# Scores of a chunked scan: the causal mask moved into the exponent, written by a fill and an accumulating transfer

## The chip, the core and the metric

The kernel runs on one core of a Trainium2 chip. A core has a matrix engine (TensorE, PE in the profile; its weight loads are PEld), a vector engine (VectorE, DVE), an activation engine (ScalarE, ACT), GpSimd (POOL) and SyncE (SP). SP, ACT and POOL each issue transfers (DMAs) in the order of their own instructions, and sixteen DMA engines that all of them share move the data. The metric is the device time of one execution in microseconds. Lower is better.

## What is computed

One layer of a hybrid decoder: token mixing by causal pooling and by a Mamba-2 scan side by side, gated and merged, then an MLP. 512 tokens plus 16 meta tokens, width 1024, everything in float32. The part that matters here is the scan, cut to its diagonal part and its output:

```python
a_cs = jnp.cumsum(a_dt, axis=2)                       # running sums within a chunk of 128
mask = jnp.tril(jnp.ones((CHUNK, CHUNK), dtype=bool))[:, :, None, None]
diff = a_cs[:, :, :, None] - a_cs[:, :, None, :]
lmat = jnp.exp(jnp.where(mask, diff, -jnp.inf))
cb = jnp.einsum("bclgn,bcsgn->bclsg", cf, bf)
y_diag = jnp.einsum("bclsg,bclsgr,bcsgrp->bclgrp", cb, lmat, xdt)
...
y_off = jnp.einsum("bclgn,bcgrpn,bclgr->bclgrp", cf, prev, jnp.exp(a_cs))
y = (y_diag + y_off).reshape(bsz, lp, SSM_HEADS, SSM_HEAD_DIM)[:, pad:]
```

For every pair of positions l >= s in a chunk, the score is `cb` times the exponential of the difference of two running sums; for l < s it is zero. There are 8 groups of 4 heads and 4 chunks of 128 positions.

## The kernel before

**Stages.** In the profile, the first 61 us are the norm, the step sizes `dt` and the first projections; 61 to 475 us is the scan over the eight groups; after it come the pooling branch, the merge and, from about 690 us, the MLP. Matmuls on TensorE run in a split form (a high and a low part of each float32 operand), which is why a weight block `raw` arrives by SP (L95), is cast by ACT to `whi` (L111) and gives `wlo` by a subtraction on DVE (L113).

**The scan.** For each group g, `ssd(g)` is a generator that computes the scan of that group, and it is woven with `group_proj(g + 1)`, which projects the next group's `bt`, `ct`, `xc` and `z` from weight blocks. `weave` pulls one step of each in turn, and a third generator issues sums of weights on POOL (L774 to L783) behind small marker copies (`seen`, L797); in the first four groups a fourth one forms sums of `u` (`rau`, `rbu`, loaded on POOL at L903, summed by DVE at L911 to L914). The instructions of one engine run in the order in which the framework put them: it plans that order from priorities and estimated durations, within the order that `tc.issue_after` and the helper `after` ask for. An engine that waits for one instruction holds all that are behind it.

**One group's scores.** The tile `abc` has one buffer, 128 partitions x 4 heads x 512 positions, 1 MB. POOL loads the running sums of the group's four heads into it, the same on every partition (L599). The load can start when the previous group's last `py` matmul (L691), which reads that buffer, is done. Then:

- ACT forms `eb = exp(abc)`, two instructions of 64 partitions each, so that the two heads of a pair lie above each other (L633); they stand behind the Silu of `xc` in the first four groups (`x_ready`) and behind that of `z` in the last four (`z_ready`, L584). ACT loads a table when the kind of function changes (`ACT_TABLE_LOAD`): Silu, Sqrt and Exp are of different kinds.
- The difference to the partition's own running sum (`dtok[:, 1]`) is clamped from above at zero: for two heads by ACT with a Relu of the negated difference (L638), for two by DVE with a subtraction and a minimum (L641), in blocks of 128x128.
- `decay` takes the exponentials of both halves (L644, L645). In the last group it stands behind the copy `st0` (L667).
- PE computes `pc`, the products of `bt` and `ct` (L656); DVE multiplies them by `tri`, the 0/1 mask, into `cbm` (L658).
- DVE multiplies the decayed scores by `cbm` over the heads (L676), and PE uses them in `py` (L691), beside `po` (L685), which takes the carried states `st`.
- DVE puts `po * eb + py` and the gates together in `yt` (L694 to L698). ACT squares it (L703) into a tile `sqg` that shares the one buffer of `eb`; its last reader is L331.

`tri` is made once, at the start, by POOL and is 1 where the position of the row is not behind that of the column. `dtok` and its companions are made once in `dt_out`.

Of the kernel before, what the change touches and what calls it, by code (L numbers as in the profile page):

```python
# [11 lines left out]
AF = mybir.ActivationFunctionType  # L12
ALU = mybir.AluOpType

P = 128
# [6 lines left out]
G = 8  # L22
R = 4
# [26 lines left out]
X_PAIRS = (4, 5, 6, 7)  # L50
# [14 lines left out]
def kernel(ctx: ExitStack, tc, xT, x, w, fx, f1, f2, vec, fnw, out):  # L65
    nc = tc.nc
    act, dve, pe, pool = nc.scalar, nc.vector, nc.tensor, nc.gpsimd
# [33 lines left out]
    def after(*ins):  # L101
        st = ExitStack()
        for i in ins:
            if i is not None:
                st.enter_context(tc.issue_after(i.ins))
        return st
# [36 lines left out]
    def mm3s(ps, pairs, first=True, last=True):  # L143
# [4 lines left out]
        for n, ((ah, al), (bh, bl)) in enumerate(pairs):  # L148
# [9 lines left out]
    tri = const.tile([P, P], F32, name="tri")  # L158
    pool.affine_select(out=tri, in_=ones_f, compare_op=ALU.is_ge, fill=0.0, base=0,
                       pattern=[[1, P]], channel_multiplier=-1)  # L160
    eps = const.tile([P, 1], F32, name="eps")
    dve.memset(eps, EPS)
    vs = const.tile([P, V_N], F32, name="vs")
# [5 lines left out]
    dtok = const.tile([P, 2, 4, HEADS], F32, name="dtok")  # L169
# [183 lines left out]
    for i in range(2):  # L353
        pb = psum1(f"pb1_{i}")
        c = slice(3 * i, 3 * i + 3)
# [14 lines left out]
    for c in range(4):  # L370
        r = slice(c * H, (c + 1) * H)
# [22 lines left out]
    acs_d = dram.tile([H, SEQ], F32, name="acs_d")  # L394
    for c in range(4):
        nc.gpsimd.dma_start(acs_d[:, c * P : (c + 1) * P], acs[c * H : (c + 1) * H, :P])
    def dt_out():

        sel = pre.tile([P, 2, P], F32, tag="wdt", name="sel")
        dve.tensor_copy(sel[:, 0, :], ident[:, P - 1 : P].to_broadcast([P, P]))  # L400
        dve.tensor_copy(sel[:, 1, :], ident[:, NM - 1 : NM].to_broadcast([P, P]))
        pt = psum1("pt_dt")
        for j, src in enumerate((dt, acs)):
            pe.transpose(pt[:, j * P : (j + 1) * P], src[:, :P], ident)
            pe.transpose(pt[:NM, 256 + j * H : 256 + (j + 1) * H], src[:H, P:], ident[:H, :H])
        dve.tensor_copy(dtok.rearrange("p a c h -> p (a c h)"), pt[:, :256])
        dve.tensor_copy(dtm.rearrange("p a h -> p (a h)"), pt[:NM, 256 : 256 + 2 * H])
        pq = psum1("pq_dt")
        pe.matmul(pq[:, :128], sel[:, 0, :], dtok[:, 1, :, :].rearrange("p c h -> p (c h)"),
                  start=True, stop=True)  # L410
        pe.matmul(pq[:NM, 128 : 128 + H], sel[:NM, 1, :NM], dtm[:, 1, :], start=True, stop=True)
        fl = lambda t: t.rearrange("p c h -> p (c h)")
        dve.tensor_tensor(fl(dec), pq[:, :128], fl(dtok[:, 1, :, :]), op=ALU.subtract)
        dve.tensor_tensor(wmeta[:NM], pq[:NM, 128 : 128 + H], dtm[:, 1, :], op=ALU.subtract)
        act.activation(fl(dec), fl(dec), AF.Exp)
        act.activation(wmeta[:NM], wmeta[:NM], AF.Exp)
        dve.tensor_tensor(wmeta[:NM], wmeta[:NM], dtm[:, 0, :], op=ALU.mult)
        act.activation(fl(cdec), pq[:, :128], AF.Exp)


    u_d = [dram.tile([P, L], F32, name=f"u_d{k}") for k in range(NK)]
# [10 lines left out]
    x_ready, z_ready, filled = {}, {}, {}  # L432
# [158 lines left out]
    def ssd(g, cur):  # L591

        xc, bt, ct, zt = cur
        hs = slice(R * g, R * g + R)
# [1 line left out]
        ctok = lambda c: slice(c * P, (c + 1) * P)  # L596
        flat = lambda t: t.rearrange("p r d -> p (r d)")
        abc = gs.tile([P, R, SEQ], F32, tag="abc", name=f"abc{g}")
        abc_load[g] = nc.gpsimd.dma_start(abc, acs_d[hs, :].partition_broadcast(P))  # L599

        xdt = gs.tile([P, 4, R, 64], F32, tag="xdt", name=f"xdt{g}")
        btok = gs.tile([P, 4, P], F32, tag="btok", name=f"btok{g}")
# [23 lines left out]
        if g == G - 1:  # L626
            yield
        eb = gs.tile([P, 2, SEQ], F32, tag="eb", name=f"eb{g}")
        ap = abc.rearrange("p (i j) l -> p i j l", j=2)
        for j in range(2):  # L630
            js = slice(64 * j, 64 * j + 64)
            with after((z_ready if g in X_PAIRS else x_ready)[g], late_cast[0] if g == G - 1 else None):
                act.activation(eb[js, :, :], ap[js, :, j, :], AF.Exp)  # L633
        dm = abc.rearrange("p r (c l) -> p r c l", c=4)
        for r in range(R):
            for c in range(4):
                if r < 2:
                    act.activation(dm[:, r, c, :], dm[:, r, c, :], AF.Relu, scale=-1.0,  # L638
                                   bias=dtok[:, 1, c, R * g + r : R * g + r + 1])
                else:  # L640
                    dve.tensor_scalar(dm[:, r, c, :], dm[:, r, c, :], dtok[:, 1, c, R * g + r : R * g + r + 1],  # L641
                                      0.0, op0=ALU.subtract, op1=ALU.min)
        def decay():
            act.activation(abc[:, :2], abc[:, :2], AF.Exp, scale=-1.0)  # L644
            return act.activation(abc[:, 2:], abc[:, 2:], AF.Exp)  # L645


        if g < G - 1:
            done[g] = decay()
        mark[0] = xdt[:, 0, 0, :1]  # L650
        yield

        pc = psum1(f"pcb{g}")
        with tc.issue_after(filled[g].ins) if g in filled else nullcontext():
            for c in range(4):
                pe.matmul(pc[:, c * P : (c + 1) * P], bt[:, tok(c)], ct[:, ctok(c)], start=True, stop=True)  # L656
        cbm = gs.tile([P, 4, P], F32, tag="cbm", name=f"cbm{g}")
        dve.tensor_tensor(cbm, pc.rearrange("p (c l) -> p c l", c=4),  # L658
                          tri.unsqueeze(1).to_broadcast([P, 4, P]), op=ALU.mult)
        st = [gs.tile([P, R, 64], F32, tag=f"st{c}", name=f"st{c}_{g}") for c in range(4)]  # L660
        pss = [psum1(f"pst{g}_{b}") for b in range(2)]
        pv = [pss[c // 2][:, (c % 2) * 256 : (c % 2) * 256 + 256] for c in range(4)]
# [11 lines left out]
        for rs_ in ((slice(0, 2), slice(2, R)) if g == G - 1 else (slice(0, R),)):  # L674
            n = rs_.stop - rs_.start
            masked[g] = dve.tensor_tensor(dm[:, rs_], dm[:, rs_], cbm.unsqueeze(1).to_broadcast([P, n, 4, P]),  # L676
                                          op=ALU.mult)
# [4 lines left out]
        for i in range(2):  # L682
# [5 lines left out]
            for c in range(4):  # L688
                for j in range(2):
                    r = 2 * i + j  # L690
# [937 lines left out]
    c = NC - 1  # L1628
# [203 lines left out]
```

## Time and profile before

| | |
|---|---|
| Median of 3 runs | 1004.51 us (1001.51 to 1004.57) |
| The profiled execution | 1003.26 us, its span 1001.6 us |
| TensorE clock granted | 0.999 |
| PE busy | 989.0 us, 99% of the span |
| DVE / ACT / POOL busy | 804.2 / 602.9 / 121.9 us |
| Moved by DMA | 184.52 MB, mean 184 GB/s |

The profile is one execution. A group row gives line, engine, operation, output<-inputs, shapes and count, then busy time and the mean of one; a row of the timeline gives start, duration, engine, line, operation, and, in brackets, how long the engine stood idle before it and what released it. A row of waits gives who waited for whom: total us, how often, the longest. A row of windows gives the stretch, its length, busy time (and count) of PE, PEld, DVE, ACT and POOL, the granted clock, the share of the DMA engines and GB/s. Matmuls overlap one another, so a PE that counts as busy is close to, but not exactly, a PE at work all the time. The span of a POOL transfer is the time of issuing it; when it has landed is told separately.

### The profile page before, as it was taken

How to read it: one execution, taken by the hardware profiler on the slowest of the kernel's cores; microseconds unless marked ns; L12 is line 12 of the kernel's file. 1: busy time of each engine (PE TensorE's matmuls, PEld its weight loads, DVE VectorE, ACT ScalarE, POOL GpSimd, SP SyncE). 2: the span in 40 equal slices, each digit the busy share in tenths (PEclk: the TensorE clock that was granted, in tenths of full speed). 3: DMA queues.
4: the chain of work that ended last, by engine and by line, in shares of the span. 5: the costliest groups of instructions: out<-in, count | busy, mean ns of one | idle time of the engine just before them, and what ended most of it. 6: DMA issues, size and time to landing. Idle time of an engine off the chain costs nothing.

```text
span 1001.6 us, 15673 instructions
## 1 busy us (share of the span) xinstructions
PE 989.0 (99%) x6035; PEld 873.4 (87%) x6035; DVE 804.2 (80%) x1162; ACT 602.9 (60%) x855; POOL 121.9 (12%) x215
## 2 busy tenths in 40 slices
PE   9999999999999999999999999999999999999997
PEld 7889898989889999978898888888889999999986
DVE  7977997879855888978789667876988878888885
ACT  7657749494924658574345443377666666656654
POOL 0010321211212312223200001121000000000000
PEclk9999999999999999999999999999999999999999
DMA  7374868676798849678823732889354464454332
GB/s 245 89 254 140 265 182 238 195 192 199 221 262 265 232 122 278 211 161 172 286 68 127 252 101 77 259 232 323 88 197 149 142 194 138 157 185 151 129 106 84
DMA packets 61803, 184.52 MB, mean 184 GB/s; under 512 B 7072, under 2 KB 8416, under 8 KB 60704
## 3 DMA queue, kind: packets, MB, share of 16 engines
q1 hardware_dynamic: 39456, 109.00, 33.3%
q0 software_dynamic: 18240, 67.51, 26.4%
q10 hardware_dynamic: 4032, 7.00, 1.9%
q8 instruction: 47, 0.77, 0.3%
q14 instruction: 28, 0.23, 0.1%
HBM read 173.13 MB, written 58.59 MB: 231 GB/s over the span
## 4 chain that ended last, share of the span: by engine, by line
PE 84%; DVE 7%; ACT 4%; DMA 3%; issue 1%; SPq 0%; ACTq 0%; DVEq 0%
PE px L1451 8%; PE px L215 7%; PE alpha L1519 6%; PE pz L215 6%; PE px L1454 4%; PE px L218 4%; PE pgp L215 3%; PE alpha L1522 3%; PE pz L218 3%; PE pgs L215 3%; DMA raw<-in_w 2%; PE pqx L506 2%; PE py L691 2%; PE pgp L218 2%; PE pso L146 1%; PE wo_alpha L1213 1%
## 5 line engine op out<-in xcount | busy, mean ns | idle before, releaser
L113 DVE TENSOR_TENSOR wlo<-raw,whi 128x1024 fp32r<-128x1024 f32 (+2 forms) x88 | 102.2, 1171 | 45.0 <-ACT whi L111 29.7
L111 ACT CAST whi<-raw 128x1024 fp32r<-128x1024 f32 (+2 forms) x88 | 87.2, 1012 | 64.0 <-DMA raw<-in_w 15.8
L215 PE MATMUL px<-uh,whi 128*128 128x264 f32 (+1 forms) x320 | 81.1, 291 | 0.0
L218 PE MATMUL px<-ul,whi 128*128 128x264 f32 (+1 forms) x320 | 78.7, 284 | 0.0
L1226 DVE TENSOR_TENSOR ht<-ht,alpha 128x1024 f32<-128x1024 f32 x35 | 42.7, 1220 | 29.1 <-PE alpha L1519 29.1
L215 PEld LDWEIGHTS px<-uh,whi 128*128 128x128 f32 x320 | 60.5, 189 | 1.1 <-issue 0.9
L1149 ACT CAST shi<-rawf 128x1024 fp32r<-128x1024 f32 x42 | 44.2, 1053 | 28.0 <-PE alpha L1522 18.4
L218 PEld LDWEIGHTS px<-ul,whi 128*128 128x128 f32 x320 | 60.2, 188 | 0.4 <-issue 0.2
L1519 PE MATMUL alpha<-shi,hh 128*128 128x512 f32 x140 | 55.3, 395 | 0.7 <-DVE ht L1226 0.6
L1522 PE MATMUL alpha<-shi,hl 128*128 128x512 f32 x140 | 54.7, 391 | 0.0
L1150 DVE TENSOR_TENSOR slo<-rawf,shi 128x1024 fp32r<-128x1024 f32 x42 | 51.2, 1219 | 0.6 <-ACT shi L1149 0.6
L1454 PE MATMUL px<-vsl,shi 128*128 128x256 f32 x192 | 47.4, 280 | 0.0
L1451 PE MATMUL px<-vsh,shi 128*128 128x256 f32 x192 | 47.4, 281 | 0.0
L215 PE MATMUL pz<-uh,whi 128*128 128x512 f32 x112 | 43.8, 391 | 1.7 <-DVE xc L440 1.7
L218 PE MATMUL pz<-ul,whi 128*128 128x512 f32 x112 | 43.6, 390 | 0.0
L215 PE MATMUL px<-uh,wlo 128*128 128x264 f32 (+1 forms) x320 | 42.0, 283 | 0.0
L215 PEld LDWEIGHTS px<-uh,wlo 128*128 128x128 f32 x320 | 40.0, 188 | 0.0
L1519 PE MATMUL alpha<-slo,hh 128*128 128x512 f32 x140 | 37.4, 389 | 0.0
L1451 PEld LDWEIGHTS px<-vsh,shi 128*128 128x128 f32 x192 | 36.2, 188 | 0.9
L1454 PEld LDWEIGHTS px<-vsl,shi 128*128 128x128 f32 x192 | 36.1, 188 | 0.9
L1454 PE MATMUL px<-vl,shi 128*128 128x256 f32 x144 | 36.1, 283 | 0.0
L1451 PE MATMUL px<-vh,shi 128*128 128x256 f32 x144 | 36.0, 282 | 0.0
(599 smaller groups left out, 3068.3 us busy)
## 6 DMA issues: line engine op xcount, KB each, us to landing
raw<-in_w SPq DMA_DIRECT2D x96, 512.0 KB, 4.6
f_t<-in_f POOLq DMA_DIRECT2D x38, 512.0 KB, 7.5
f_s<-in_f POOLq DMA_DIRECT2D x26, 512.0 KB, 7.0
b<-in_f SPq DMA_DIRECT2D x21, 512.0 KB, 4.4
rawf<-in_f SPq DMA_DIRECT2D x36, 256.0 KB, 3.0
rawf<-f_t SPq DMA_DIRECT2D x36, 256.0 KB, 3.1
abc<-acs_d POOLq DMA_DIRECT2D x8, 1024.0 KB, 8.3
f_t<-f_t POOLq DMA_DIRECT2D x12, 512.0 KB, 6.7
```

Source lines behind the costliest of these rows:

```text
L111: act.copy(hi[:, c], raw[:, c])
L113: dve.tensor_tensor(lo[:, c], raw[:, c], hi[:, c].bitcast(F32), op=ALU.subtract)
L215: pe.matmul(o, wt, rhs[0][k][:, c], start=part == 0 and k == 0, stop=part == 1 and k == NK - 1)
L218: mm[0] = pe.matmul(o, wt, rhs[1][k][:, c], start=False, stop=False)
L506: at = pe.matmul(o, wk, f[k][0], start=start and not low and k == 0, stop=stop and low == 1 and k == 3, skip_group_check=True)
L1149: splits.append((act.copy(hi, src), dve.tensor_tensor(lo, src, hi.bitcast(F32), op=ALU.subtract)))
L1150: dve.tensor_tensor(lo, src, hi.bitcast(F32), op=ALU.subtract)))
L1226: added[0] = dve.tensor_tensor(o, o, src, op=op)
L1451: pe.matmul(ps, m, f[k][0], start=start and not low and k == 0, stop=stop and low == 1 and k == 3, skip_group_check=True)
L1454: pe.matmul(ps, m, f[k][1], start=False, stop=False, skip_group_check=True)
L1519: pe.matmul(ps[t], hh[:, p, seg, st], m, start=bool(first and not low and p == 0), stop=bool(last and low and p == 1), skip_group_check=True)
L1522: pe.matmul(ps[t], hl[:, p, seg, st], m, start=False, stop=False, skip_group_check=True)
```

## The change

The mask goes from a product into the exponent. `tri` becomes 0 where it was 1, and -1e30 where it was 0. For each group POOL first fills `abc` with `tri`, repeated for 4 heads x 4 chunks, from SBUF, and then adds the running sums to it with an accumulating transfer. The sign of the stored own sums (`dtok[:, 1]`) is turned once, so that ACT can take exp(abc + bias) block by block: 16 exponentials with a bias per group take the place of eight Relus, eight DVE subtractions and two wide exponentials. All of them, in every group, now stand behind `z_ready`. `eb` gets its own two loads of the running sums, 64 partitions each, and one exponential on all partitions, which follows the decays in the program (in the last group it comes before them, and `decay` still stands behind `st0`). `cbm` is a plain copy by ACT of `pc`.

```diff
@@ -158,6 +158,7 @@
     pool.affine_select(out=tri, in_=ones_f, compare_op=ALU.is_ge, fill=0.0, base=0,
                        pattern=[[1, P]], channel_multiplier=-1)
+    dve.tensor_scalar(tri, tri, 1.0, 1e30, op0=ALU.subtract, op1=ALU.mult)
@@ -416,6 +417,7 @@
         act.activation(fl(cdec), pq[:, :128], AF.Exp)
+        dve.tensor_scalar(fl(dtok[:, 1, :, :]), fl(dtok[:, 1, :, :]), -1.0, None, op0=ALU.mult)
@@ -596,7 +598,9 @@
         abc = gs.tile([P, R, SEQ], F32, tag="abc", name=f"abc{g}")
-        abc_load[g] = nc.gpsimd.dma_start(abc, acs_d[hs, :].partition_broadcast(P))
+        nc.gpsimd.dma_start(abc.rearrange("p r (c l) -> p (r c) l", l=P),
+                            tri.unsqueeze(1).to_broadcast([P, 4 * R, P]))
+        abc_load[g] = nc.gpsimd.dma_start(abc, acs_d[hs, :].partition_broadcast(P), accum_op=ALU.add)
@@ -626,27 +630,26 @@
         eb = gs.tile([P, 2, SEQ], F32, tag="eb", name=f"eb{g}")
-        ap = abc.rearrange("p (i j) l -> p i j l", j=2)
         for j in range(2):
-            js = slice(64 * j, 64 * j + 64)
-            with after((z_ready if g in X_PAIRS else x_ready)[g], late_cast[0] if g == G - 1 else None):
-                act.activation(eb[js, :, :], ap[js, :, j, :], AF.Exp)
+            nc.gpsimd.dma_start(eb[64 * j : 64 * j + 64, :, :],
+                                acs_d[hs, :].rearrange("(i j) l -> j i l", j=2)[j].partition_broadcast(64))
         dm = abc.rearrange("p r (c l) -> p r c l", c=4)
-        for r in range(R):
-            for c in range(4):
-                if r < 2:
-                    act.activation(dm[:, r, c, :], dm[:, r, c, :], AF.Relu, scale=-1.0,
-                                   bias=dtok[:, 1, c, R * g + r : R * g + r + 1])
-                else:
-                    dve.tensor_scalar(dm[:, r, c, :], dm[:, r, c, :], dtok[:, 1, c, R * g + r : R * g + r + 1],
-                                      0.0, op0=ALU.subtract, op1=ALU.min)
+
         def decay():
-            act.activation(abc[:, :2], abc[:, :2], AF.Exp, scale=-1.0)
-            return act.activation(abc[:, 2:], abc[:, 2:], AF.Exp)
-
+            for r in range(R):
+                for c in range(4):
+                    with after(z_ready[g]):
+                        at = act.activation(dm[:, r, c, :], dm[:, r, c, :], AF.Exp,
+                                            bias=dtok[:, 1, c, R * g + r : R * g + r + 1])
+            return at
+
+        def in_decay():
+            with after(z_ready[g], late_cast[0] if g == G - 1 else None):
+                act.activation(eb, eb, AF.Exp)
 
         if g < G - 1:
             done[g] = decay()
+        in_decay()
@@ -655,8 +658,7 @@
-        dve.tensor_tensor(cbm, pc.rearrange("p (c l) -> p c l", c=4),
-                          tri.unsqueeze(1).to_broadcast([P, 4, P]), op=ALU.mult)
+        act.copy(cbm.rearrange("p c l -> p (c l)"), pc)
```

## The prediction

> **What bounds the kernel now.** I read the page first, then the waits of PE between 60 and 470 us (the scan over the eight groups), then the scan as one stretch of the windows.
>
> ```profile
> span 1001.6 us, 15673 instructions
> PE 989.0 (99%) x6035; PEld 873.4 (87%) x6035; DVE 804.2 (80%) x1162; ACT 602.9 (60%) x855; POOL 121.9 (12%) x215
> ...
> PE 84%; DVE 7%; ACT 4%; DMA 3%; issue 1%; SPq 0%; ACTq 0%; DVEq 0%
> ...
> raw<-in_w SPq DMA_DIRECT2D x96, 512.0 KB, 4.6
> ...
> f_t<-f_t POOLq DMA_DIRECT2D x12, 512.0 KB, 6.7
> ```
>
> ```profile
> PE pz L215 <- DVE xc L440: 1.7, 1, 1.7
> PE psp L146 <- ACT sp L868: 1.4, 1, 1.4
> PE po L685 <- ACT st L667: 0.2, 1, 0.2
> ```
>
> ```profile
> 61.00:475.00 414.00, 410.52 (x2721) 368.06 (x2720) 329.74 (x508) 266.10 (x369) 92.67 (x163) 1.00 0.75 211
> ```
>
> PE is busy for 99% of the span and 410.5 of the scan's 414 us. It waits three times there, 1.7 + 1.4 + 0.2 = 3.3 us in all. The change leaves every matmul as it is, so those 3.3 us are about all that it can win. What it can lose is not bounded in this way: PE takes its work in order, and one late `py` (L691, which reads the decayed scores `abc`) stops everything behind it. So the question is how late the scores become and how much room they have.
>
> **What the vector engines save.** The view of the tile `abc` (min/median/max ns) and two lines beside it:
>
> ```profile
> L641 DVE TENSOR_SCALAR abc<-abc,dtok x64: 189/281/385, 82.6 to 443.2; 128x128 f32<-128x128 f32 x64
> L638 ACT ACTIVATE abc<-abc,dtok x64: 387/390/416, 83.6 to 442.0; 128x128 f32<-128x128 f32 x64
> L633 ACT ACTIVATE eb<-abc x16: 1056/1060/1067, 81.5 to 437.9; 64x1024 f32<-64x1024 f32 x16
> L599 POOL DMA_DIRECT2D abc<-acs_d x8: 535/567/577, 61.8 to 415.8; - x8
> L645 ACT ACTIVATE abc<-abc x8: 1038/1046/1060, 86.0 to 444.5; 128x1024 f32<-128x1024 f32 x8
> ...
> DMA to landing us min/median/max: 5.1/8.3/11.4
> ```
>
> ```profile
> L658 DVE TENSOR_TENSOR cbm<-pcb,tri x8: 680/692/692, 82.0 to 443.4; 128x512 f32<-128x512 f32 x8
> ```
>
> ```profile
> L608 ACT COPY btok<-ptb x8: 561/580/592, 73.0 to 433.9; 128x512 f32<-128x512 f32 x8
> ```
>
> In each group DVE loses eight subtractions, at most 8 x 0.28 = 2.2 us, and the masking product of 0.69 us: 2.9 us at most. ACT loses two `eb` exponentials (2.1), eight Relus (2.46 as a run in the timeline rows below, 0.31 each) and two wide exponentials (2.1, less the overlap: 2.0): 6.6 us. It gains 16 biased exponentials on the same 128x128 blocks, 16 x 0.31 = 4.9, one `eb` exponential on all partitions (1.06) and the copy of `pc` (0.58, as the 128x512 copy of L608): 6.5 us. So ACT is even. The one-time rewrite of `tri` and the sign change of `dtok` are two 128x128 DVE operations, 0.3 us each, before the scan; nothing waits closely on them and I count nothing.
>
> **What the loads cost.** One load of 1 MB becomes a chain: fill `abc` with the mask, wait until it has landed, add the sums. The trace has the same wait already, in POOL's weight sums, at half the size:
>
> ```profile
> 114.76 0.90 POOL L782 DMA_DIRECT2D fx_t<-in_fx  x1
> ...
> 122.42 0.81 POOL L783 DMA_DIRECT2D fx_t<-fx_t  x1 [6.54 <-DMA fx_t<-in_fx]
> ```
>
> An accumulation issued behind a plain copy stood 122.42 - 114.76 = 7.7 us after it. Second leg: a 512 KB accumulation lands in 6.7 us (page), so 1 MB takes between the 8.3 us of a plain MB and twice 6.7, 13.4; I take 10, nearer the plain row, since most of a landing doesn't grow with the size. First leg: a plain MB takes 8.3 us (5.1 to 11.4), but the fill is cut into 128 x 16 = 2048 pieces of 512 bytes instead of 128 rows of 8 KB. No row shows a transfer of so many pieces from POOL. From below: the store of the sums has 32 rows.
>
> ```profile
> L396 POOL DMA_DIRECT2D acs_d<-dacs x4: 518/524/680, 49.1 to 50.8; - x4
> ```
>
> From 32 to 128 rows the instruction grows from 524 to 567 ns, 0.45 ns a piece, so 1920 more cost 0.9 us. From above: all 567 ns in proportion to the pieces, 4.4 ns each, 8.5 us. The ends are a factor of ten apart; I take the middle in ratio, 2.8 us. The chain is then 8.3 + 2.8 + 0.8 (issue of L783) + 10 = 21.9 us from the issue, where the load took 8.3. With the ends of each leg it runs from 5.1 + 0.9 + 0.8 + 8.3 = 15.1 to 11.4 + 8.5 + 0.8 + 13.4 = 34.1.
>
> The Trainium skill prices a POOL transfer at 2.0 us plus bytes over 436 GB/s (DMA: Bandwidth & Descriptors, Anatomy of one DMA), 4.4 us for 1 MB, and a chain of about 10 us. The 5.1 to 11.4 us measured here are above it at every load, because the weights share the engines, so the measurement decides.
>
> **Where that is late.** The load is issued when the previous group's `py` has released `abc`; the exponentials now all stand behind the gate's Silu and the table load. First group, second, and seventh:
>
> ```profile
> 61.77 0.57 POOL L599 DMA_DIRECT2D abc<-acs_d  x1 [10.49 <-DVE xt L425]
> ```
>
> ```profile
> 80.18 1.28 ACT L633 ACT_TABLE_LOAD   x1
> 81.47 2.14 ACT L633 ACTIVATE eb<-abc 64x1024 f32<-64x1024 f32 x2
> 83.64 2.46 ACT L638 ACTIVATE abc<-abc,dtok 128x128 f32<-128x128 f32 x8
> ```
>
> ```profile
> 88.02 2.29 DVE L676 TENSOR_TENSOR abc<-abc,cbm 128x2048 f32<-128x2048 f32 x1 [2.83 <-ACT abc L644]
> ```
>
> ```profile
> 90.68 0.55 PE L691 MATMUL py<-abc,xdt 128*64 128x128 f32 x6
> ```
>
> First group: ACT would start at 81.47, 19.7 us after the issue; the chain needs 21.9, so 2.2 late. From there to the product (L676) it is 6.5 us before and after if `eb` and the copy stand ahead of it as they are written. The product ended at 90.3, `py` began at 90.7: 0.4 of room, 1.8 us of stall.
>
> ```profile
> 98.69 0.57 POOL L599 DMA_DIRECT2D abc<-acs_d  x1 [2.06 <-PE py L691]
> ```
>
> ```profile
> 120.05 2.45 ACT L638 ACTIVATE abc<-abc,dtok 128x128 f32<-128x128 f32 x8
> 122.52 1.28 ACT L645 ACT_TABLE_LOAD   x1
> ```
>
> ```profile
> 132.90 1.09 PE L691 MATMUL py<-abc,xdt 128*64 128x128 f32 x16
> ```
>
> Second group: exponentials from 120.05 + 1.28 = 121.3; the chain lands at 120.6. Not late. They end at 126.2, `eb`, the copy and two casts bring the product to 129 and its end to 131.3, ahead of 132.9.
>
> ```profile
> 373.37 0.58 POOL L599 DMA_DIRECT2D abc<-acs_d  x1 [0.58 <-PE py L691]
> ```
>
> ```profile
> 393.37 2.14 ACT L633 ACTIVATE eb<-abc 64x1024 f32<-64x1024 f32 x2
> ...
> 401.50 0.36 ACT L667 COPY st<-pst 128x256 f32<-128x256 f32 x1
> ```
>
> ```profile
> 403.53 2.29 DVE L676 TENSOR_TENSOR abc<-abc,cbm 128x2048 f32<-128x2048 f32 x1
> ```
>
> ```profile
> 405.92 0.33 PE L691 MATMUL py<-abc,xdt 128*64 128x128 f32 x2
> ```
>
> Seventh group: 20.0 us from issue to first exponential, so 1.9 late, and 5.0 if the first leg takes the view's maximum of 11.4. DVE came to the product 2.0 us after ACT was done (403.53 against 401.50), which swallows that much: 0 to 3.0 us of stall, I take 1.5.
>
> The other groups have more room; the nearest of them, and the last:
>
> ```profile
> 143.67 0.54 POOL L599 DMA_DIRECT2D abc<-acs_d  x1
> ```
>
> ```profile
> 167.79 2.46 ACT L638 ACTIVATE abc<-abc,dtok 128x128 f32<-128x128 f32 x8
> ```
>
> ```profile
> 415.80 0.57 POOL L599 DMA_DIRECT2D abc<-acs_d  x1 [3.19 <-PE py L691]
> ```
>
> ```profile
> 442.33 0.35 ACT L667 COPY st<-pst 128x256 f32<-128x256 f32 x1
> ```
>
> 24.1 us and 26.5 us against 21.9: not late. But in the last group all 16 exponentials stand behind the `st` copy, where two wide ones (2.0 us) stood: 2.9 us more ahead of the `sp` copies for which PE waits 1.4 already. The Relus that go move the copy forward by up to 2.5 us. I add 1.0 us, between -1.4 and +2.9.
>
> On POOL the added wait holds what is queued behind it for about 11 us a group: the two `eb` loads, the `rau`/`rbu` loads, the weight sums behind their markers (L797). The sums stand still on such markers already:
>
> ```profile
> POOL seen L797 <- ACT bt L442: 90.3, 7, 16.0
> ```
>
> That waiting hides it; without it, each group's sums would come 11 us later, before a reader that comes groups later. For `eb` I count nothing: it is exponentiated last and used after `po`. (Its buffer is also that of the squared outputs, so its load waits for the previous group's L331 too.) Finally the DMA engines, 75% busy over the scan, get 1 MB of fill, 0.5 MB of `eb` and a dearer addition in each group, and the weight blocks on SP land later. If one takes half as long again, 4.6 to 6.9 us, that costs PE nothing where the block was early and 2.3 us where it was just in time; I take 1.0, between 0 and 2.3.
>
> Sum: 1.8 + 1.5 + 1.0 + 1.0 = 5.3 us. The profiled execution took 1003.26 us (span 1001.6), which makes 1008.6; the median of the runs stands 1.25 above it, so 1009.8. Bounds: with the chain at 15.1 us no group is late, and what is left of the sum is -1.4 to 5.2; at 34.1 the first group stalls 34.1 - 19.7 - 0.4 = 14.0, the seventh 34.1 - 20.0 - 2.0 = 12.1, the second 34.1 - 22.6 - 1.6 = 9.9, some 36 us, but only with both legs and the pieces at their worst together.
>
> **Rivals.** (1) *Hidden anyway.* If pieces cost 0.9 us and the legs run near 5.1 and 8.3, the chain is 15 us, under each group's 19.7, and PE sees nothing: 1004.5. For it: one load did land in 5.1. Against: the engines become busier, and half of the loads took over 8.3. The skill's fit above would give this. (2) *Descriptor writing at full price*, 8.5 us: the chain is 27.6. First group 7.9 - 0.4 = 7.5; second 126.3 - 121.3 = 5.0 late, less 1.6 of room (131.3 to 132.9), 3.4; seventh 7.6 - 2.0 = 5.6; third 143.67 + 27.6 - 169.1 = 2.2 late, of which I take 1.0; last 1.5. With 1.0 for the weights 20.0: 1024.5. For it: nobody in this trace has asked POOL for 2048 pieces. Against: its instruction hardly grows between 32 and 128. The skill also holds that POOL cannot write descriptors while DVE is in a two-port mode (SBUF — State Buffer, SBUF: two separate sides), which would stretch it more; L599's 535 to 577 ns under a DVE 80% busy show no such thing. (3) *Faster.* The chain is hidden and DVE's 2.9 us shift its backlog: the wait at L215 on L440, behind a DVE that stood 2.83 us before the product in group one, and both waits on ACT in the last group go. Price 3.3 us, 1001.2; it decides only if the chain stays under 19.7 us. (4) *The order moves*: the issue order on the engines is worked out from estimated durations, so new operations may put a cast or an evacuation behind the waiting exponentials in any group, 1 to 2 us each, 10 to 16 us: about 1017.
>
> **How the numbers follow.** Forecast 0.36, rivals 0.22, 0.18, 0.15, 0.09. Own range of the forecast 1006 to 1014; the whole from 1001, which takes in most of rival 3, to 1024. 0.3%, about 3 us, is what a measurement of this kernel can tell from no change. Faster by more: rival 3, 0.15. Within: rival 1 and a small part of the forecast, 0.25. Slower: the rest, 0.60.
>
> **What would show it.** Landing of the second transfer of `abc` 20 to 24 us after the first's issue; ACT idle before the first exponential of groups one and seven, ended by that landing; PE waiting at `py` on the product there, and nowhere else by more than 1 us; DVE's busy time in the scan down by about 20 us, ACT's level. The forecast is wrong if PE's waits in the scan stay under 4 us, or if they stand at weight blocks instead of `py`.

## The result and the profile after

The changed kernel takes 1049.56 us (median of 4 runs, 1045.3 to 1053.17) where the kernel before took 1003.18 beside it (1001.51 to 1004.57): a ratio of 1.0463, 95% interval 1.0442 to 1.0485. The forecast was 1009.8 in a range of 1001 to 1024. The sign was right, the size seven times too small: 6.6 us over the kernel before instead of 46.

The profiled execution took 1045.3 us, the lowest of the four, its span 1043.6, at a granted clock of 0.982. From its page: the span, the busy times, the shares of the chain that ended last, and the transfers into `abc`. The new line numbers are L601 for the fill, L603 for the addition, L634 for the loads of `eb`, L642 for the 16 exponentials, L648 for the exponential of `eb`, L661 and L669 for the copies of `pc` and of the first state.

```profile
span 1043.6 us, 15711 instructions
PE 1001.5 (96%) x6035; PEld 883.2 (85%) x6035; DVE 787.3 (75%) x1092; ACT 600.3 (58%) x902; POOL 140.3 (13%) x239
...
PE 66%; DMA 11%; DVE 6%; ACT 4%; issue 4%; POOL 1%; ACTq 0%; POOLq 0%; DVEq 0%
...
raw<-in_w SPq DMA_DIRECT2D x96, 512.0 KB, 5.3
...
abc<-tri POOLq DMA_DIRECT2D x8, 1024.0 KB, 6.9
abc<-acs_d POOLq DMA_DIRECT2D x8, 1024.0 KB, 11.1
```

The 42.0 us that the span grew by are PE's alone, and they have two parts. PE is busy 12.5 us longer (1001.5 against 989.0) with the same 6035 matmuls, so some of them ran slower. And it is idle 29.5 us longer (42.1 against 12.6). DVE and ACT both have less to do than before, 16.9 and 2.6 us. So no vector engine became the bound. The part of the chain of waits that runs through transfers went from 3% to 11%.

Where PE stands still, by its waits from 60 to 530 us (who waited for whom, us in total, times, longest):

```profile
PE psp L882 <- ACT yh L723: 11.4, 1, 11.4
PE py L693 <- issue: 6.8, 5, 1.8
PE po L687 <- ACT st L669: 5.7, 2, 3.4
PE po L687 <- DVE st L675: 3.8, 1, 3.8
PE pst L667 <- DVE xdd L628: 2.1, 2, 1.6
```

Only the second row has the place that was forecast (`py`). The first and largest is a projection, `psp`, that has nothing to do with the scores; the next two are `po`, which waits for the carried states. None of the three reads `abc`. Behind the first of them and the first `po` row stands ACT, and there one instruction; the `po` row that waits for DVE has another story, told below. The timeline of ACT in the second group:

```profile
120.83 3.62 ACT L642 ACTIVATE abc<-abc,dtok 128x128 f32<-128x128 f32 x12
124.36 1.12 ACT L723 CAST yh<-yt 128x512 fp32r<-128x512 f32 x2
125.39 1.28 ACT L642 ACTIVATE abc<-abc,dtok 128x128 f32<-128x128 f32 x4
132.11 1.06 ACT L648 ACTIVATE eb<-eb 128x1024 f32<-128x1024 f32 x1 [5.45 <-DMA eb<-acs_d]
133.08 0.77 ACT L439 ACTIVATE bt<-px,vs 128x528 f32<-128x528 f32 x1
133.75 0.57 ACT L661 COPY cbm<-pcb 128x512 f32<-128x512 f32 x1
```

The scores are done at 126.7, in good time. Then ACT stands 5.45 us before the exponential of `eb`, whose load has not landed, and behind it in the order stand the copy of `pc`, without which DVE can't make the masked product, and the state copy. `eb` itself is needed by nobody yet. The last group shows the same thing at its worst, on three engines:

```profile
460.71 0.89 POOL L634 DMA_DIRECT2D eb<-acs_d  x1
...
461.45 0.80 POOL L776 DMA_DIRECT2D f_t<-in_f  x1
...
471.82 0.84 POOL L785 DMA_DIRECT2D f_t<-f_t  x1 [9.57 <-DMA f_t<-in_f]
472.38 0.91 POOL L634 DMA_DIRECT2D eb<-acs_d  x1
...
481.16 1.28 ACT L648 ACT_TABLE_LOAD   x1 [10.92 <-DMA eb<-acs_d]
482.45 1.06 ACT L648 ACTIVATE eb<-eb 128x1024 f32<-128x1024 f32 x1
483.42 1.12 ACT L723 CAST yh<-yt 128x512 fp32r<-128x512 f32 x2
...
484.07 2.08 PE L882 MATMUL psp<-yh,whi 128*128 128x512 f32 x4 [11.38 <-ACT yh L723]
```

POOL issues one half of the load of `eb` at 460.71. Then an accumulating weight sum (L785) waits 9.57 us in its queue for the transfer that it adds to, and the other half goes out at 472.38 and lands at 481.1. ACT waits for it 10.92 us, with the casts of `yh` behind it, and PE waits 11.38 for these casts.

The 3.8 us of `po` on DVE are in the third group, and there `eb` held up nobody. ACT's timeline:

```profile
171.70 1.06 ACT L111 CAST whi<-raw 128x1024 fp32r<-128x1024 f32 x1 [3.63 <-DMA raw<-in_w]
175.54 1.05 ACT L111 CAST whi<-raw 128x1024 fp32r<-128x1024 f32 x1 [2.78 <-DMA raw<-in_w]
...
181.75 4.79 ACT L642 ACTIVATE abc<-abc,dtok 128x128 f32<-128x128 f32 x16
186.45 1.04 ACT L648 ACTIVATE eb<-eb 128x1024 f32<-128x1024 f32 x1
...
188.54 0.37 ACT L669 COPY st<-pst 128x256 f32<-128x256 f32 x1
```

ACT stood 6.4 us for two weight blocks and was then busy without a pause up to the state copy, from which DVE makes the next states. Over the scan (60 to 480 us) ACT's casts waited 9.5 us for `raw` and 10.2 for `rawp`, the blocks that `whip` is cast from; in the kernel before it was 1.5 and nothing. So the transfers on SP became late as well: those of `raw` that were issued in the scan land in 6.6 us (median), 4.9 before.

How long the transfers took, from the view of the tile `abc` (ns min/median/max of the issuing instruction, first and last start) and the row of `eb` among the DMA issues (KB each, median us to landing):

```profile
L601 POOL DMA_DIRECT2D abc<-tri x8: 1180/1202/1221, 60.9 to 447.3; - x8
L603 POOL DMA_DIRECT2D abc<-acs_d x8: 866/886/972, 73.4 to 456.9; - x8
```

```profile
eb<-acs_d POOLq DMA_DIRECT2D x16, 256.0 KB, 12.4
```

A load of `eb` takes 12.4 us for a quarter of a megabyte, longer than either megabyte of `abc`.

### The profile page after: what moved, and what is told of

Its sections match the earlier page's. It is cut to its first block, busy times and chain, and to the rows that moved or that the text cites. A ratio compares the mean times of both kernels' runs of the same rounds, so it can differ in the third digit from the quotient of the medians.

```text
span 1043.6 us, 15711 instructions
## 1 busy us (share of the span) xinstructions
PE 1001.5 (96%) x6035; PEld 883.2 (85%) x6035; DVE 787.3 (75%) x1092; ACT 600.3 (58%) x902; POOL 140.3 (13%) x239
## 2 busy tenths in 40 slices
DMA packets 65259, 197.10 MB, mean 189 GB/s; under 512 B 7456, under 2 KB 8800, under 8 KB 64160
## 4 chain that ended last, share of the span: by engine, by line
PE 66%; DMA 11%; DVE 6%; ACT 4%; issue 4%; POOL 1%; ACTq 0%; POOLq 0%; DVEq 0%
PE px L1453 8%; PE alpha L1521 6%; PE px L1456 4%; PE alpha L1524 3%; DMA eb<-acs_d 3%; PE px L216 3%; DMA f_t<-in_f 3%; DMA raw<-in_w 3%; PE pgs L216 2%; PE py L693 2%; DMA rawp<-fx_t 1%; PE wo_alpha L1215 1%; PE po L687 1%; PE px L219 1%; PE pf L146 1%
## 5 line engine op out<-in xcount | busy, mean ns | idle before, releaser
L442 DVE SCALAR_TENSOR_TENSOR bt<-px,vs,bt 128x527 f32<-128x527 f32 (+2 forms) x21 | 15.9, 757 | 30.7 <-ACT bt L439 30.7
L642 ACT ACTIVATE abc<-abc,dtok 128x128 f32<-128x128 f32 x128 | 38.7, 388 | 0.1
## 6 DMA issues: line engine op xcount, KB each, us to landing
abc<-acs_d POOLq DMA_DIRECT2D x8, 1024.0 KB, 11.1
```

What stands on the lines that cost most here:

```text
L642: at = act.activation(dm[:, r, c, :], dm[:, r, c, :], AF.Exp, bias=dtok[:, 1, c, R * g + r : R * g + r + 1])
```

## The experiments

All are variants of the kernel before or of the changed kernel. The ratios are to the kernel before, run beside them; its medians lay between 1002.3 and 1003.6. Two suspects stood at the start. **The chain**: fill and addition, one behind the other, make `abc` late and hold up what is behind them in POOL's queue. **The loads of `eb`**: two more transfers a group, for which ACT waits in the middle of its order, cost the time by themselves.

**1. The chain alone, in the kernel before.** `abc` is filled with zeros and the sums are added; `eb`, the Relus and the masked product stay as they were.

```diff
+    zer = const.tile([P, P], F32, name="zer"); dve.memset(zer, 0.0)
-        abc_load[g] = nc.gpsimd.dma_start(abc, acs_d[hs, :].partition_broadcast(P))
+        nc.gpsimd.dma_start(abc.rearrange("p r (c l) -> p (r c) l", l=P),
+                            zer.unsqueeze(1).to_broadcast([P, 4 * R, P]))
+        abc_load[g] = nc.gpsimd.dma_start(abc, acs_d[hs, :].partition_broadcast(P), accum_op=ALU.add)
```

> The kernel before, with one thing of the change alone: abc is filled with zeros and the sums are added to it. Theory A (the eb loads and their queueing on POOL make the loss): within 8 us of before, 1001 to 1011. Theory B (the chain of fill and addition makes it, as predicted): 1020 or more, with ACT idle before L633-like first reads of abc and PE waiting for py. Theory C (the order on ACT, sixteen exponentials and eb ahead of the cbm and st copies): 1001 to 1011 too, since that order is not in it.

Measured: 1029.68 us, 1.0256 (1.0233 to 1.028), in the range of theory B. ACT waits 17.2 us for `abc` in this kernel, in three groups, the longest 7.8, and 5.9 for weight blocks; PE's largest wait is 6.1 us at `ptx`, which reads neither.

**2. The loads of `eb` alone, in the kernel before.** The edit leaves the exponential of `eb` ahead of the Relus in the text of the kernel; it no longer reads `abc`, so no data hold the Relus behind it.

```diff
-                act.activation(eb[js, :, :], ap[js, :, j, :], AF.Exp)
+            nc.gpsimd.dma_start(eb[64 * j : 64 * j + 64, :, :],
+                                acs_d[hs, :].rearrange("(i j) l -> j i l", j=2)[j].partition_broadcast(64))
...
+            act.activation(eb, eb, AF.Exp)
```

> The kernel before, with the two eb loads on POOL and one eb exponential alone. Theory A: 1020 or more, ACT waiting for the eb landing by 10 us or more in sum, longest in the last group behind a weight sum. Theory B: no change, 1001 to 1006. Theory C: eb stays ahead of the Relus here, so whatever its landing costs ACT shows directly, but without a late abc: 1005 to 1015.

Measured: 1035.78 us, 1.0338 (1.0309 to 1.0367). ACT's waits in this kernel:

```profile
ACT L633 <- DMA eb<-acs_d: 15.2, 3, 5.3
ACT abc L638 <- DMA abc<-acs_d: 13.0, 6, 3.7
ACT eb L633 <- DMA eb<-acs_d: 2.9, 1, 2.9
```

Each part is dear alone, 26 and 32 us, and together they cost 46. This run isn't the loads alone, though. Against what was expected, the Relus begin ahead of the exponential of `eb` in all eight groups (in the second at 104.4 us, with `eb` at 129.5; before, `eb` at 113.2 and the Relus at 120.1), and ACT waits 13.0 us for `abc` there, although its plain load lands in 6.8. What share of the 32 us is this new order can't be told. So the next runs take parts out of the changed kernel.

**3. The changed kernel without the fill.** One plain load of the sums; it leaves out the mask (and the sign change of `dtok`, so that the exponents stay finite). The loads of `eb` stay.

```diff
-        nc.gpsimd.dma_start(abc.rearrange("p r (c l) -> p (r c) l", l=P),
-                            tri.unsqueeze(1).to_broadcast([P, 4 * R, P]))
-        abc_load[g] = nc.gpsimd.dma_start(abc, acs_d[hs, :].partition_broadcast(P), accum_op=ALU.add)
+        abc_load[g] = nc.gpsimd.dma_start(abc, acs_d[hs, :].partition_broadcast(P))
```

> The changed kernel with a plain load of the sums in place of fill and addition, and the sign of dtok left as it was, so the mask is left out and the exponents stay negative. The eb loads stay. If the two transfers add up, it gives back what the chain cost alone, 26 us: 1020 to 1026. If both delays stand behind one another in the same queue and hide each other, it gives back less: 1030 to 1040.

Measured: 1013.51 us, 1.0098 (1.008 to 1.0116), below both ranges that were expected. 36 of the 46 us are gone. Its DMA issues:

```profile
abc<-acs_d POOLq DMA_DIRECT2D x8, 1024.0 KB, 6.9
eb<-acs_d POOLq DMA_DIRECT2D x16, 256.0 KB, 6.6
```

The same loads of `eb` land in 6.6 us instead of 12.4. So the chain makes `eb` late, and not only `abc`. The one long wait left, 4.8 us of `psp` on `yh` in the last group, is the one above in small.

**4. The arithmetic alone.** As run 3, but `eb` is made from `abc` as in the kernel before, so there is no new transfer at all. It leaves out the mask.

> The changed kernel's arithmetic alone: 16 biased exponentials, the plain copy of the C*B product on ACT, one plain load of the sums, eb made from abc as in the kernel before, and no new transfer. It leaves out the mask. It closes the ladder of runs: this, then eb loaded by transfers of its own (1013.5), then the fill ahead of the load (1035.3), then the addition (1049.6). Theory A (the loss is in the transfers): 1000 to 1006 us, since DVE has lost 2.9 us a group and ACT is even, and no gap of PE over 2.3 us in the scan. Rival (the new order of the exponentials on ACT costs by itself, as the 1011.4 of the kernel with the mask added by DVE might mean): 1008 to 1013, with PE's gaps at the products of the scan.

Measured: 1004.66 us (10 runs), 1.002 (1.0007 to 1.0032): about 2 us slower, less than the 3 us that the prediction set as the limit to no change. Its page has `DVE 786.5`, 17.7 us less than before. The new form of the exponentials wins nothing, and costs 3 us at most. A gap of PE of 2.96 us before `pz`, where 2.3 was expected as the most, brought no half clock (more on this at runs 11 and 12).

**5. Fill, then a plain load.** The changed kernel with all its transfers and their waits, but the second one writes over the mask instead of adding to it. It leaves out the mask (and the sign change).

```diff
-        abc_load[g] = nc.gpsimd.dma_start(abc, acs_d[hs, :].partition_broadcast(P), accum_op=ALU.add)
+        abc_load[g] = nc.gpsimd.dma_start(abc, acs_d[hs, :].partition_broadcast(P))
```

> The changed kernel with its fill kept, but the second transfer loads the sums plainly over the mask instead of adding them (the sign change of dtok goes too, so that the exponents stay finite): it leaves out the mask. The same number of transfers, the same wait of the second for the first; only the addition becomes a write. Theory A (the waiting: two transfers one behind the other, with the eb loads behind both in POOL's queue, make abc and eb late): the second transfer lands some 8 us after its issue instead of 11.1, the eb loads in 9 to 12 us, and most of the loss stays: 1030 to 1045 us. Theory B (the addition is what is dear: it reads and writes abc, and holds up the eb loads behind it): abc lands 6 to 8 us after its issue and eb as without the fill, in about 6.6 us, PE has no gap over 3 us, and the time comes near the kernel without the fill (1013.5): 1014 to 1025.

Measured: 1035.26 us, 1.0316 (1.0296 to 1.0337), in the range of theory A.

```profile
abc<-tri POOLq DMA_DIRECT2D x8, 1024.0 KB, 7.3
abc<-acs_d POOLq DMA_DIRECT2D x8, 1024.0 KB, 8.1
eb<-acs_d POOLq DMA_DIRECT2D x16, 256.0 KB, 10.5
```

Runs 4, 3, 5 and the changed kernel make a ladder, each with one thing more in its text: 1.0020 with the arithmetic, 1.0098 with the loads of `eb`, 1.0316 with the fill ahead of the load, 1.0463 with the addition in place of the write. At 1003 us the steps are 2.0, 7.8, 21.9 and 14.7 us. (Between the first two the exponential of `eb` also moves behind the scores.) The framework plans the order of each kernel anew, so a step can hold a change of order too. The last step doesn't: by the two traces POOL and PE run the same instructions in the same order, and ACT and DVE too but for the sign change of `dtok` and its neighbour. The largest step is the fill in front; that the second transfer adds is worth another third of the loss, and with it that transfer lands 3.0 us later (11.1 against 8.1) and `eb` 1.9.

**6. The exponential of `eb` behind the state copy.** The changed kernel with all its transfers; one instruction of ACT moves.

```diff
-        in_decay()
         mark[0] = xdt[:, 0, 0, :1]
...
         y_first[g] = st0 = act.copy(flat(st[0]), pv[0])
+        with tc.issue_after(st0.ins):
+            in_decay()
```

> The changed kernel, with the eb exponential moved behind the copy of the first state (and so behind that of cbm). Theory A, if the loss comes from ACT standing in order before eb lands: PE's 11.4 us wait in the last group and the waits for po go, 1049 falls to 1015 to 1028. Theory B: no change within 6 us, 1043 to 1053. Theory C: falls by a third to a half, 1025 to 1035, because the sixteen exponentials still stand ahead.

Measured: 1027.36 us, 1.0243 (1.0228 to 1.0259), 22 us less than the changed kernel, inside the ranges of both theory A and theory C. `eb` still lands in 12.4 us (median), so what the edit changes is who stands behind it. The framework's order changed elsewhere too (in the second group PE does all sixteen `py` in one go, in the changed kernel fourteen and two), so not all of the 22 us need be the one move. PE is busy 992.5 us instead of 1001.5, and the time at half clock is 17 us instead of 34. PE's largest waits are now

```profile
PE po L688 <- DVE st L676: 10.7, 5, 3.8
PE py L694 <- issue: 9.9, 3, 7.9
```

and the 7.9 is the last group once more, where `eb` now stands ahead of the scores instead of the casts. The wait moved, and where it moved to a place with less behind it, it became cheaper.

**7. The loads of `eb` on SP's queue**, away from the addition (`nc.sync` in place of `nc.gpsimd` at L634).

> The changed kernel, with the eb loads issued by SP instead of POOL. Theory A: they land in 4 to 7 us and behind no weight sum; the wait at L648 falls from 18 us to under 4; 1015 to 1030. Theory B: 1043 to 1053 as the changed kernel. Theory C: 1035 to 1045. SP holds the weight blocks in the same queue, so if the eb loads wait there for their buffer, weight blocks come late and the time does not fall.

Measured: 1043.57 us, 1.0397 (1.0375 to 1.0419), 6 us less where theory A gave 20 or more. They land in 10.3 us there, not in the 4 to 7 expected. Leaving the queue brought back 2.1 of the 5.8 us by which `eb` is late; that the rest is contention for the sixteen shared engines would fit, but no run measured it alone. The Trainium skill says that within one queue of one DMA engine the descriptors (the pieces of a transfer) start in order, though they overlap (DMA: Bandwidth & Descriptors, Two DMAs through the same engine are not ordered); no run here shows single descriptors.

**8. The loads of `eb` as early as they can go** (a higher priority at L634).

```diff
+            with tc.high_priority(100000):
                 nc.gpsimd.dma_start(eb[64 * j : 64 * j + 64, :, :], ...
```

> The changed kernel, with the eb loads given the highest priority, so that in the last group POOL issues both before the weight sum that waits 9.6 us. Theory A1 (the queue on POOL is what makes eb late): the 10.9 us wait of ACT and the 11.4 us wait of PE in the last group go, and with them the stretch at half clock behind it: 1049 falls by 12 to 18, to 1031 to 1037. Theory A2 (eb is late because its packets stand behind the addition's in the DMA engines, in every group): no more than 6 us.

Measured: 1046.08 us, 1.0416 (1.0392 to 1.0441), in the range of theory A2. The last group's wait falls from 11.4 to 5.4 us, since both halves are now issued ahead of the weight sum. But in the first group they go ahead of the fill, which starts at 73.5 instead of 60.9, and there `py` waits 4.5. The median landing is 12.9 us.

**9. Both, 6 and 8**, with the last group's `eb` behind the scores.

> The changed kernel with the eb loads first and the eb exponential behind the copies of cbm and st, in the last group behind the decays too. What is left is the chain of fill and addition: if the eb part is repaired by that, 1012 to 1020, with no PE wait over 3 us in the last group; if the chain alone costs what it costs in the kernel before (26 us), 1026 to 1032.

Measured: 1030.32 us, 1.0267 (1.0226 to 1.0309). No better than 6 alone: `py` waits 4.0 in the first group and `po` 8.9 in all.

**10. The mask added by DVE.** The changed kernel's arithmetic without a new transfer: plain load, `eb` from `abc`, and one DVE addition of `tri` to `abc`, 128x2048.

```diff
+        rows = abc.rearrange("p r (c l) -> p (r c) l", l=P)
+        dve.tensor_tensor(rows, rows, tri.unsqueeze(1).to_broadcast([P, 4 * R, P]), op=ALU.add)
```

> The mask in the exponent without any new transfer: plain load, eb from abc as before, the mask added by DVE over all of abc, sixteen exponentials with a bias, cbm copied by ACT. If the loss comes from the transfers alone (theories A and B): 1000 to 1008. If the new order on ACT behind z_ready costs by itself (theory C): 1012 or more, with waits of PE for st and py.

Measured: 1011.42 us, 1.0075 (1.0055 to 1.0095), between the two ranges expected. This is the cheapest form of the idea that was run with the mask in it, and it still loses: the addition gives back the DVE time that the change saved (804.9 us busy, 804.2 before), and the pooling branch behind the scan waits 5.0 us for DVE once.

**11 and 12. A delay without a transfer.** The 12.5 us by which PE's busy time grew were still open. In the trace of the changed kernel the granted clock falls to one half in five stretches between 136 and 488 us, 34 us in all; before, it stood at full speed through the whole scan. Each stretch begins inside a gap in PE's work or at most 2.1 us after one. To see whether the gap does this or the transfers do, DVE multiplies the masked scores of the kernel before by 1.0, once or three times, in the first and the seventh group.

```diff
+        for _ in range(1 if g in (0, 6) else 0):        # 3 in run 12
+            masked[g] = dve.tensor_scalar(abc, abc, 1.0, None, op0=ALU.mult)
```

> The kernel before, in which DVE multiplies the masked scores by 1.0 once more in the first and the seventh group, between the masked product and py: a delay in front of PE without any transfer, 128x2048 each, 1 to 2.3 us, in the two groups that had 0.4 and 0.1 us of room in the trace of before. Clock theory (gaps of PE over about 2.3 us are followed by 3.4 to 10.2 us at half clock): the gaps stay under it, the clock stays at 1.0 all through the scan, and the time grows by the gaps alone: 1004 to 1008 us. Rival (the half clock belongs to the load of the chip, or to the transfers, not to the gaps): the same here.

> The same with three such multiplications in the two groups, so 3 to 7 us of delay each. Clock theory: two gaps of PE of 3 to 6 us, each followed by 3.4 to 10.2 us at half clock, and the time grows by the gaps and half of the half-clock time, 10 to 20 us together: 1013 to 1024. Rival (the gaps do not bring the half clock): the clock stays at 1.0 in the scan, and the time grows by the gaps alone, 6 to 12 us: 1009 to 1015.

Measured: 1005.48 us (10 runs), 1.0021 (1.0007 to 1.0034), and 1009.38 us, 1.006 (1.0044 to 1.0077). Both delays are 1.22 us a piece and mostly disappeared: PE's wait at `py` was 0.5 and 1.6 us. So the sizes were expected wrongly: run 12 lies at the low end of what the rival gave, and below what the clock theory gave, because the two gaps of 3 to 6 us never came about. But the delay came out in another place: DVE was late with `xc`, and PE's wait there, 1.7 us before, became 2.7 and 3.2, and both times a stretch of 6.8 us at half clock follows it, against the rival, and in run 11 against the expectation that the gaps would stay short enough. In run 11, from the timeline and then from the windows (stretch, length, busy time and count of PE, PEld, DVE, ACT, POOL, clock, DMA share, GB/s):

```profile
105.77 0.76 PE L215 MATMUL pz<-uh,whi 128*128 128x512 f32 x1 [2.65 <-DVE xc L440]
106.13 0.70 DVE L923 TENSOR_TENSOR t1l<-rbu,t1h 128x528 fp32r<-128x528 f32 x1
106.33 0.63 PE L218 MATMUL pz<-ul,whi 128*128 128x512 f32 x1
```

```profile
95.00:102.00 7.00, 7.00 (x67) 6.71 (x66) 7.00 (x13) 2.45 (x4) 3.71 (x4) 1.00 0.60 171
102.00:105.00 3.00, 1.12 (x10) 0.91 (x8) 3.00 (x5) 1.64 (x3) 0.83 (x3) 1.00 1.06 281
105.00:112.00 7.00, 6.23 (x15) 4.90 (x16) 7.00 (x11) 1.70 (x2) 1.60 (x3) 0.51 0.91 321
112.00:119.00 7.00, 7.00 (x33) 5.76 (x32) 4.21 (x10) 6.01 (x8) 2.37 (x5) 1.00 1.04 277
```

and the same stretch of the kernel before, whose gap ends at 105.13:

```profile
105.00:112.00 7.00, 6.87 (x30) 5.73 (x31) 7.00 (x10) 3.92 (x6) 2.12 (x4) 1.00 0.87 282
```

After the gap PE gets through 15 matmuls in 7 us where it got through 30, each 0.63 us instead of 0.40, at a clock of 0.51. The stretch is 6.8 us long, so it costs 3.4 at most. And it is not always there: of run 11's ten executions four had a mean clock of 0.999 or 1.000 and took 1003.1 to 1004.5 us, six had 0.995 to 0.997 and took 1005.4 to 1007.9; the medians, 1003.9 and 1006.8, are 2.9 us apart. Only the profiled one of the six has a trace, and the kernel before, run beside it, varies as well (four of thirteen at 0.997, 1004.3 to 1005.0 us), so that the six had this stretch is likely, not shown. In run 12 all four had 0.995 or 0.996. So no new transfer is needed for the half clock; a gap can do it, and need not, as run 4 shows.

## Why the prediction was wrong

**The step that failed** is "For `eb` I count nothing: it is exponentiated last and used after `po`." Its reason looks at who reads `eb`. What counts is who stands behind its exponential on ACT: the copy of `pc`, the state copy, the casts of `yh`, none of which reads `eb`. The changed kernel's waits at `psp` (11.4) and at `po` on ACT's states (5.7) come from there, and moving that one instruction in ACT's order (run 6) gives back 22 us, though `eb` and the addition land as late as before the move (12.4 and 11.1 us). The reason given doesn't hold in all groups either: in the last one the kernel's text puts the exponential of `eb` ahead of the scores, and in the first one the trace does (82.5 against 86.8 us). And `eb` isn't the whole: run 1 has no load of `eb` and loses 26 us.

**The step that fed it** is the one on POOL: the wait of the addition holds the two `eb` loads, and "that waiting hides it". The trace of before showed that the weight sums can wait; PE has no long wait that names them. But `eb` stands in the same queue and can't: behind the addition it lands in 12.4 us instead of 6.6 (run 3), and in the last group it also stands behind a weight sum that waits 9.57. The sum of the prediction listed `eb` among what is held and then priced it at zero.

**The term that was mis-sized** is the one for the weight blocks, 1.0 us, "between 0 and 2.3". It looks only at PE. ACT's casts waited 19.7 us for blocks in the scan instead of 1.5, and in the third group two such waits stand straight ahead of PE's 3.8 us at `po`, with 3.4 us at half clock behind them. What these waits cost in all, no run measured alone.

**The term that was missing** is the clock. Every wait was counted at its own length. In the changed kernel 34 us at half clock lose another 17 us of work at most (some of it falls into the gaps themselves); the busy time grew by 12.5 us. Runs 11 and 12 show the mechanism without the transfers.

Point by point:

- **3.3 us is all that can be won**: nothing here speaks against it. The arithmetic alone (run 4) is at 1.002, with 17.7 us less on DVE. Rival 3 (faster) fails even where nothing is late.
- **DVE loses 2.9 us a group at most, ACT is even**: right. DVE's busy time fell by 16.9 us (2.1 a group), ACT's by 2.6 in all.
- **The chain is 21.9 us from issue to landing**: close in sum, by luck in part. In the eight groups it took 23.7, 21.3, 19.4, 18.3, 15.9, 18.4, 23.4 and 17.2 us, a mean of 19.7. Its terms: 6.9 for the first leg (I took 8.3), 11.1 for the addition (10), and for the 2048 pieces 1.20 us of issue against 0.57, 0.6 us where I took 2.8 from a range of 0.9 to 8.5. The 23.7 of the first group has a term that the sum lacks: the fill had landed at 67.5, but the addition went out at 73.4, as the two `eb` loads stood ahead of it on POOL and waited 10.1 us for DVE. By the fit of the Trainium skill (DMA: Bandwidth & Descriptors, Anatomy of one DMA) I estimate the chain at about 10 us; all eight lie above it.
- **First group 1.8 us, seventh 1.5**: the places are right, in the first by luck. PE stood 1.2 us at `py` there, but ACT didn't wait for the landing (84.6 us): it had `eb`, a Silu and three table loads to do, and began the scores at 86.8. In the seventh ACT waited 5.0 us for `abc` and 2.0 more for `eb`, and PE had two gaps of 3.7 and 1.9 us from one matmul's start to the next.
- **Second group not late**: right for the scores, as ACT's timeline shows, and of no use, because `eb` was late behind them: PE's gaps there were 2.6 and 2.1 us.
- **Last group 1.0, for ACT's order**: it was 11.4, and by `eb`, not by the 16 exponentials.
- **Weight loads 1.0**: over the whole kernel the blocks land in 5.3 us instead of 4.6, and PE's own waits in the scan name no block of more than 0.4 us. But ACT waited for them, as said above, so the term was too small.
- **The rivals.** Hidden anyway (1) would need a chain under 19.7 us in each group; it was over it in three. Descriptor writing (2) came nearest in time, 1024.5, for a reason that didn't hold. The order that moves (4), at about 1017, named the right kind of thing, a copy or a cast behind a waiting exponential, but as an accident of planning; it stood in the text of the kernel.
- **What would show it**: a landing 20 to 24 us after the issue came in three groups of eight; ACT's wait for `abc` in the seventh only; and "PE waiting at `py` and nowhere else by more than 1 us" is what the page refutes in one look.

That the whole loss is accounted for can't be said. The split between waits and half clock differs from run to run, and what share of the slower `eb` is the queue and what the shared engines stays open. A second buffer for `abc`, which would let the fill start a group earlier, was not tried. Nor was the planned order held fixed, save in the last step of the ladder.

## What to carry to other kernels

When a transfer becomes later, price it at the instruction that waits for it: list everything behind that instruction in its engine's order, and behind the transfer in its queue, whether or not it reads the data. A value that is needed last should also be waited for last. And on a kernel that keeps PE at 99%, a stall of 2 us and one of 4 are not of one kind: behind the second, 3.4 us or more at half clock are likelier.

## What the runs showed of the hardware

**Half clock after a gap.** In the traces here gaps of PE (start to start) up to 2.21 us, standing alone, left the clock at full. Between that and 3 us it went either way: one of 2.22 us in run 9 and one of 2.31 us in run 5 were followed by 3.4 us at half clock, one of 2.31 us in run 9 by none. The gap before `pz` of 2.93 to 2.98 us brought nothing in run 4, 3.4 us at half clock in runs 3 and 10, and 6.8 in run 11; the 11.8 us gap of the changed kernel brought 10.2. In the changed kernel two gaps of about 2 us, 9 us apart (237.9 and 247.0), were followed by 3.4. Shorter gaps close together went either way too: 1.63 and 1.18 us in run 7 were followed by 3.4, 1.84 and 1.18 in run 5 by none. The lengths are steps of 3.4 us. The Trainium skill advises no idle gaps of PE over about 3 us (TensorE: Matmul & The Clock Gate, Why this matters for your kernels); gaps just under that, at `pz`, brought the half clock three times out of four here.

**A small load behind a large one.** 256 KB took 6.6 us behind a plain megabyte, 10.5 behind a fill and a plain megabyte, and 12.4 behind a fill and an addition. Its size says nothing of its time.

**The fill is cheap to issue.** A fill that the kernel writes as 2048 pieces of 512 bytes cost POOL's instruction 1.20 us against 0.57 for 128 rows, and it lands in 6.9 us, as fast as a plain megabyte does in run 3. That it moves as so many pieces is not shown: by the pages, run 5 with its eight fills has 65259 packets and run 3 without them 63083, which is 272 for a fill.
